# A third buffer for weight loads: taken over later, and its first load pinned in the queue

## The chip, the cores and the metric

The kernel runs on one core of a Trainium2 chip. The metric is the device time of one execution in microseconds. It is given as the median of several runs. One further execution was taken with the hardware profiler, and every row shown here comes from it.

## What is computed

One step of a hybrid encoder layer for 1024 prompt tokens and 32 sample tokens that share all weights, with model width 1024. Cut to the main lines, the reference is

```python
h = rms_norm(x, g_mix)
q, k, v, ch, cb, cc, ga, gb = split(h @ w_in)
a = window_attention(q, k, v) @ w_attn_out
bo = (cb * causal_conv3(cc * ch)) @ w_conv_out
x = x + (sigmoid(ga) * a + sigmoid(gb) * bo) @ w_mix_out
x = x + cross_attention(rms_norm(x, g_cross) @ w_cq, mem_k, mem_v) @ w_co
x = x + square(relu(rms_norm(x, g_mlp) @ w_up)) @ w_down
y = rms_norm(x, g_final)
```

with outputs for the new keys, values, convolution states and memory keys and values beside `y`.

## The kernel before

**Layout.** Activations lie transposed: 128 features on the partitions, tokens along the free axis. The 1056 tokens are three chunks of 384, 384 and 288. A weight is used in blocks of 128 x 1024 floats (512 KB). Every operand is split into a high and a low part, and a product is three matmuls (high x high, high x low, low x high), so a block of 1024 x 128 weights against one chunk of 384 columns is 24 matmuls.

**How a weight comes in.** `fetch_w` (line 145) takes a raw tile and issues the load on SyncE (line 155); `issue_w` (line 158) has ScalarE cast it into `wh` (line 129 in the profile, the line of a helper's `act.copy`) and VectorE subtract to get `wl` (line 130). `wh` and `wl` have three tiles each, the raw tile `wr` has two. `next_w` keeps three weights ready when an item of the plan asks for one, so a weight is cast at most when the third weight before it has been used up. `worder` is the order of all weights, written down while the plan is made. Odd-numbered weights of conv_out, mix, cq and co have their low part stored to DRAM (line 172, `wl_d`) the first time and loaded again (line 166) for the later chunks, where only the cast (line 167) is done anew.

**The third raw tile.** While the dictionary `third` is filled, each third fetch goes into a tile `ws` of another pool instead of `wr`. In the gate stage (`gate_pair`, line 908) that pool is `Y["top"]`. After the gates it is `W["pool"]`, whose only tile is also one of the two buffers of the weight sums:

```python
if third:
    third["n"] += 1
if third and third["n"] % 3 == 0:
    raw = third["pool"].tile([P, 4, 256], F32, tag="ws", name=nm("wr3"))...
```

**The weight sums.** `sum_step` (line 702) runs on GpSimd: a piece of weights is loaded into `ws` or `xacc` by turns (line 712 or 714), four adds combine its quarters (line 719), and the sums are written to DRAM (`gsum_d`, `usum_d`, `wsum_d`; lines 723 to 725). The last pieces are parts of `w_up`, written to `usum_d`. All these steps come before `after_gates` in the plan.

**Stages around the change.** First come seven gate pairs, f from 1 to 7, each with the weights w_in 34+f, two g_sum blocks and w_in 42+f. Then `after_gates` (line 1018) fills `third` anew with the count 0. Then comes the list `trunks[0]`: conv_out 0 to 7 of chunk 0, conv_out 0 of chunk 1, and mix 0 to 7 of chunk 0. `beside` (line 1630) puts these items into the plan one by one, with extra calls after chosen items. Then follow the rest of chunk 1 beside the cross-attention of chunk 0, and so on. `do_conv_out` (line 1042) loads a part `m1_d` (line 1046), adds on GpSimd (line 1051) and splits the result for mix. `do_mix` (line 1057) loads x (line 1061) and adds it (line 1065). `mem_load` (line 1094) loads memory keys and values (lines 1076 and 1085). `open_late` empties `third` much later.

**What sets the order.** The order in which the engines get their instructions is not only the program's. A scheduler simulates the whole program while it is built and gives an engine the earliest instruction in the program whose data and tile it holds to be free at that moment; SyncE then issues its loads strictly in that order. `pin` marks an instruction: it may not be put ahead of the instruction that precedes it on its engine in the program.

Of the kernel before, what the change touches and what calls it, by code (L numbers as in the profile page):

```python
# [23 lines left out]
NF = 8  # L24
# [16 lines left out]
def hybrid_step(ctx: ExitStack, tc: tile.TileContext, io):  # L41
    nc = tc.nc
    act, dve, pool_e, pe, sp = nc.scalar, nc.vector, nc.gpsimd, nc.tensor, nc.sync
# [3 lines left out]
    def nm(s):  # L47
        uid[0] += 1
        return f"{s}_{uid[0]}"

    def opened(name, **kw):
        cm = tc.tile_pool(name=name, **kw)
        return cm, cm.__enter__()

    def closed(cm):
        cm.__exit__(None, None, None)
# [40 lines left out]
    def pin(ins):  # L97
        return tc.keep_in_program_order(ins)
# [6 lines left out]
    def tmp(n, dt=F32):  # L105
        return tp.tile([P, n], dt, tag="ct", bufs=NCT, name=nm("ct"))
# [11 lines left out]
    def item(fn, *keys):  # L118
        plan.append((fn, keys))
        worder.extend(keys)  # L120
# [11 lines left out]
    def weight(key):  # L132
        name, *at = key
        if name in ("w_down", "w_sum"):
            q, j, t = at
            return (wsum_d if name == "w_sum" else io[name])[j, t, :, :, q].rearrange("i p c -> p i c")
        if name == "g_sum":
            return gsum_d[at[0]][:, at[1]].rearrange("p h c -> p (h c)")
        src = io[name]
        for j in at:  # L140
            src = src[j]
        return src

    fetched = []
    third = {}

    def fetch_w():
# [3 lines that stand above are left out]
            raw = third["pool"].tile([P, 4, 256], F32, tag="ws", name=nm("wr3")).rearrange("p q c -> p (q c)")  # L151
        else:
            raw = wp.tile([P, 1024], F32, tag="wr", bufs=2, name=nm("wr"))
        src = weight(worder[wpos[0] + len(fetched)])
        sp.dma_start(raw.rearrange("p (i c) -> p i c", i=4) if len(src.shape) == 3 else raw, src)
        fetched.append(raw)

    def issue_w():
        if not fetched:
            fetch_w()  # L160
        raw = fetched.pop(0)
        key = worder[wpos[0]]
        hi = wp.tile([P, 1024], F32R, tag="wh", name=nm("wh"))
        lo = wp.tile([P, 1024], F32R, tag="wl", name=nm("wl"))
        if kept.get(key) is not None:
            sp.dma_start(lo.bitcast(F32), kept[key])
            act.copy(hi, raw)
        else:
            split(hi, lo, raw)
            if key in kept:  # L170
                kept[key] = dram.tile([P, 1024], F32, name=nm("wl_d"))
                sp.dma_start(kept[key], lo.bitcast(F32))
        ready.append((worder[wpos[0]], (hi, lo)))
        wpos[0] += 1
# [39 lines left out]
    def xacc_tile():  # L214
        xacc[0] = tp.tile([P, 1056], F32, tag="xacc", name=nm("xacc"))
        return xacc[0]
# [59 lines left out]
    W = {}  # L276
# [11 lines left out]
    def norm_x():  # L288
# [7 lines left out]
        def load_x():  # L296
            for c, (o, n) in enumerate(CH):
                raw = raw_tile()[:, : NF * n].rearrange("p (f t) -> p f t", f=NF)
                for h in range(4):
                    sp.dma_start(raw[:, 2 * h : 2 * h + 2], io[f"x{c}"][:, 2 * h : 2 * h + 2])  # L300
                    if c == h == 0:
                        sp.dma_start(prm, io["params"])
                        fetch_w()
                if c == 0:
                    fetch_w()
                    fetch_w()
                raws.append(raw)
# [427 lines left out]
    for i, h in enumerate(hosts):  # L735
        kv, p = i // 8, i % 8
# [54 lines left out]
    def pump(n):  # L791
        for into, at, t, get in coming:
            hi, lo = into[at] = (get(), get())
            pin(act.copy(hi, t))
            pin(dve.tensor_sub(lo, t, hi.bitcast(F32)))
        coming.clear()
        for into, at, src, cols, get in wanted[:n]:
            t = cols() if callable(cols) else tmp(cols)
            sp.dma_start(t, src)
            coming.append((into, at, t, get))  # L800
        del wanted[:n]
# [216 lines left out]
    def after_gates():  # L1018
        nonlocal m_cm, mpool, cr_cm, cr
        assert not pieces and "new" not in W  # L1020
        closed(x_cm)
        xacc_tile()
        third.update(n=0, pool=W["pool"])
        m_cm, mpool = opened("mpool", bufs=18, reuse_waits="tile")
        cr_cm, cr = opened("cross", bufs=1, reuse_waits="tile", side="right")

    item(after_gates)


# [583 lines left out]
    def cross_steps(c):  # L1613

        steps = [("call", [mem_load if c == 0 else mem_load_s])]
        steps.append(("call", [lambda: chunk_stats(c)]))
        steps.append(("items", [(do_cq(c, j), ("w_cq", j)) for j in range(2)]))
        for i, step in enumerate(cross_units(c)):
            steps.append(step)
            if i < 4 - c:  # L1620
                steps.append(("call", []))
        if c:
            steps.append(("call", []))
        steps.append(("items", [(do_co(c, 0), ("w_co", 0))]))
        steps.append(("items", [(do_co(c, 1), ("w_co", 1))]))
        if c == 0:
            steps.append(("call", [lambda: chunk_stats(c)]))
        return steps

    def beside(steps, fillers, late=()):  # L1630
        for i, filler in enumerate(fillers):
            item(*filler)
            for x in [x for at, x in late if at == i]:
                item(lambda x=x: x())
            if steps:
                kind, what = steps.pop(0)
                for x in what:
                    if kind == "items":
                        item(*x)
                    else:  # L1640
                        item(lambda x=x: x())
        return steps

    def trunk(c):
        return [(do_conv_out(c, f), ("w_conv_out", f)) for f in range(NF)] + [
            (do_mix(c, f), ("w_mix", f)) for f in range(NF)
        ]
# [3 lines left out]

    trunks = [trunk(c) for c in range(3)]
    trunks[0].insert(NF, trunks[1].pop(0))
    left = beside([], trunks[0], [(i, lambda: pump(2)) for i in range(NF)])
    item(lambda: pump(0))
    left = beside(cross_steps(0), trunks[1])

# [327 lines left out]
```

## Time and profile before

| | |
|---|---|
| median of 3 runs | 1779.99 us (1779.09 to 1783.26) |
| the profiled execution | 1778.09 us, its span 1776.3 us |
| TensorE busy | 1734.2 us, 98% |
| VectorE, ScalarE, GpSimd busy | 1184.4, 852.8 and 576.8 us |
| DMA | 349.75 MB, 197 GB/s in the mean |

Times of rows are counted from the start of the span. In a timeline row stand start, duration, engine and line, operation, tiles, and in brackets the idle time of the engine before it and what ended it. `SPq` is the SyncE queue. A row of busy times by stretch gives the stretch, its length, the busy time of PE, PEld (weight load into TensorE), DVE (VectorE), ACT (ScalarE) and POOL (GpSimd) with the number of instructions, then the granted TensorE clock, the busy share of the DMA engines and GB/s. A row of waits gives the waiting engine and line, what it waited for, and the total, count and longest in us.

### The profile page before, as it was taken

The numbers are of one execution on the slowest core, as the hardware profiler recorded it, in microseconds if no ns is written. First come the engines' busy times: TensorE is split into PE (matmuls) and PEld (weight loads), VectorE is DVE, ScalarE is ACT, GpSimd is POOL, SyncE is SP. The second block draws the span as 40 slices with busy tenths as digits, with TensorE's granted clock in tenths as the row PEclk, the third lists the DMA queues.
The fourth block names the chain that finished last, engine by engine and source line by source line (L and its number), as shares of the span: only waits on it lengthen the run. The fifth ranks groups of instructions, "written<-read, shape, count | busy, mean of one in ns | idle before, by whom it ended". The sixth has DMA issues, their size and how long they took to land.

```text
span 1776.3 us, 32569 instructions
## 1 busy us (share of the span) xinstructions
PE 1734.2 (98%) x12250; PEld 1716.3 (97%) x12250; DVE 1184.4 (67%) x2270; ACT 852.8 (48%) x1660; POOL 576.8 (32%) x651
## 2 busy tenths in 40 slices
PE   8999999999999999979999999999999999999998
PEld 8999999999999999979999989999999999999998
DVE  7776867868666647536667677786666686556575
ACT  8643534435335324324556665774444463333443
POOL 0025366543453444531225130004555510000121
PEclk9999999999999999989999998999999999999999
DMA  5333334333446888747765667575666686554554
GB/s 183 109 117 128 111 128 155 120 139 136 148 155 223 298 274 288 264 166 272 261 213 196 236 224 233 183 257 196 223 221 224 213 310 212 186 184 167 193 173 157
DMA packets 182221, 349.75 MB, mean 197 GB/s; under 512 B 19744, under 2 KB 102976, under 8 KB 181936
## 3 DMA queue, kind: packets, MB, share of 16 engines
q1 hardware_dynamic: 167008, 295.07, 49.1%
q0 software_dynamic: 15056, 52.60, 8.4%
q8 instruction: 96, 1.57, 0.4%
q14 instruction: 61, 0.50, 0.1%
HBM read 252.82 MB, written 94.19 MB: 195 GB/s over the span
## 4 chain that ended last, share of the span: by engine, by line
PE 77%; DMA 11%; POOL 6%; DVE 2%; issue 2%; ACT 2%; SPq 0%; DVEq 0%; POOLq 0%; ACTq 0%
PE acc L193 10%; PE acc L195 10%; PE acc L194 10%; PE acc L1772 6%; PE acc L1770 6%; PE acc L1771 6%; PE acc L864 5%; PE acc L866 5%; PE acc L865 5%; DMA wsum_d<-ws 3%; DMA wsum_d<-xacc 3%; POOL ws L719 2%; POOL xacc L719 2%; PE pc L864 2%; PE pc L865 2%
## 5 line engine op out<-in xcount | busy, mean ns | idle before, releaser
L129 ACT CAST wh<-wr 128x1024 fp32r<-128x1024 f32 x226 | 237.2, 1050 | 424.5 <-PE acc L1771 126.2
L130 DVE TENSOR_TENSOR wl<-wr,wh 128x1024 fp32r<-128x1024 f32 x226 | 292.5, 1294 | 140.6 <-ACT wh L129 138.6
L193 PE MATMUL acc<-X,wh 128*128 128x384 f32 (+1 forms) x864 | 281.8, 326 | 6.6 <-ACT wh L129 6.6
L194 PE MATMUL acc<-X,wh 128*128 128x384 f32 (+1 forms) x864 | 279.1, 323 | 0.0
L195 PE MATMUL acc<-X,wl 128*128 128x384 f32 (+1 forms) x864 | 278.5, 322 | 0.3 <-DVE wl L130 0.3
L269 POOL TENSOR_TENSOR xacc<-xacc,ct 128x384 f32<-128x384 f32 (+1 forms) x56 | 73.4, 1314 | 401.8 <-ACT ct L267 400.3
L193 PEld LDWEIGHTS acc<-X,wh 128*128 128x128 f32 x864 | 163.0, 189 | 7.2 <-ACT wh L129 6.6
L194 PEld LDWEIGHTS acc<-X,wh 128*128 128x128 f32 x864 | 163.1, 189 | 0.7
L195 PEld LDWEIGHTS acc<-X,wl 128*128 128x128 f32 x864 | 162.8, 188 | 0.9 <-DVE wl L130 0.8
L195 PE MATMUL acc<-Y,wl 128*128 128x384 f32 (+1 forms) x432 | 139.1, 323 | 1.8 <-DMA wl<-wl_d 1.8
L193 PE MATMUL acc<-Y,wh 128*128 128x384 f32 (+1 forms) x432 | 138.8, 323 | 0.4 <-ACT Y L774 0.4
L194 PE MATMUL acc<-Y,wh 128*128 128x384 f32 (+1 forms) x432 | 139.1, 322 | 0.0
L1770 PE MATMUL acc<-n,wh 128*128 128x264 f32 x352 | 100.2, 285 | 0.0
L1771 PE MATMUL acc<-n,wh 128*128 128x264 f32 x352 | 100.1, 284 | 0.0
L1772 PE MATMUL acc<-n,wl 128*128 128x264 f32 x352 | 100.0, 285 | 0.1
L129 ACT CAST PTh<-pt 128x512 fp32r<-128x512 f32 (+3 forms) x94 | 46.0, 516 | 111.6 <-PE pt L582 110.8
L719 POOL TENSOR_TENSOR ws<-ws 128x256 f32<-128x256 f32 x100 | 91.9, 919 | 5.6
L719 POOL TENSOR_TENSOR xacc<-xacc 128x256 f32<-128x256 f32 x100 | 87.9, 879 | 5.5 <-DMA xacc<-in_w_in 0.2
L195 PEld LDWEIGHTS acc<-Y,wl 128*128 128x128 f32 x432 | 81.1, 188 | 2.1 <-DMA wl<-wl_d 2.1
L193 PEld LDWEIGHTS acc<-Y,wh 128*128 128x128 f32 x432 | 80.9, 188 | 0.7 <-ACT Y L774 0.7
L194 PEld LDWEIGHTS acc<-Y,wh 128*128 128x128 f32 x432 | 81.1, 188 | 0.0
L864 PE MATMUL acc<-n,wh 128*128 128x264 f32 x256 | 72.9, 285 | 0.8 <-DVE Z L1502 0.8
(422 smaller groups left out, 5511.5 us busy)
## 6 DMA issues: line engine op xcount, KB each, us to landing
wr<-in_w_in SPq DMA_DIRECT2D x53, 512.0 KB, 3.7
wr<-in_w_up SPq DMA_DIRECT2D x53, 512.0 KB, 4.5
wr<-wsum_d SPq DMA_DIRECT2D x40, 512.0 KB, 3.4
wr<-in_w_conv_out SPq DMA_DIRECT2D x24, 512.0 KB, 4.3
wr<-in_w_mix SPq DMA_DIRECT2D x24, 512.0 KB, 4.8
wr<-in_w_down SPq DMA_DIRECT2D x24, 512.0 KB, 3.4
wl<-wl_d SPq DMA_DIRECT2D x18, 512.0 KB, 4.6
n_d<-Z SPq DMA_DIRECT2D x32, 264.0 KB, 4.3
```

The costliest lines, as they stand in the source:

```text
L129: act.copy(hi, src)
L130: dve.tensor_sub(lo, src, hi.bitcast(F32))
L193: pe.matmul(out, wh[:, a], hi, start=(k == 0), stop=False)
L194: pe.matmul(out, wh[:, a], lo, start=False, stop=False)
L195: pe.matmul(out, wl[:, a], hi, start=False, stop=(k == len(acts) - 1))
L719: pin(pool_e.tensor_tensor(t[:, to], t[:, x], t[:, y], op=ALU.add))
L864: pe.matmul(acc, wh[:, a], hi, start=(start and k == 0), stop=False, skip_group_check=True)
L865: pe.matmul(acc, wh[:, a], lo, start=False, stop=False, skip_group_check=True)
L866: pe.matmul(acc, wl[:, a], hi, start=False, stop=(k == 3), skip_group_check=True)
L1770: pe.matmul(a, wh[:, s], hi, start=(t == 0 and k == 0), stop=False, skip_group_check=True)
L1771: pe.matmul(a, wh[:, s], lo, start=False, stop=False, skip_group_check=True)
L1772: pe.matmul(a, wl[:, s], hi, start=False, stop=(t == 1 and k == 7), skip_group_check=True)
```

## The change

`after_gates` no longer fills `third`. It is filled, with the count 0, by an extra call behind the item of index 12 in `trunks[0]`, which is mix 3 of chunk 0. The first load into the third tile of that pool, fetch number 3 of the new count, is pinned. Up to mix 3 all fetches use the two `wr` tiles.

```diff
@@ fetch_w
-        sp.dma_start(raw.rearrange("p (i c) -> p i c", i=4) if len(src.shape) == 3 else raw, src)
+        load = sp.dma_start(raw.rearrange("p (i c) -> p i c", i=4) if len(src.shape) == 3 else raw, src)
+        if third and third["n"] == 3 and third["pool"] is W["pool"]:
+            pin(load)
         fetched.append(raw)
@@ after_gates
         xacc_tile()
-        third.update(n=0, pool=W["pool"])
         m_cm, mpool = opened("mpool", bufs=18, reuse_waits="tile")
@@ the plan
     trunks[0].insert(NF, trunks[1].pop(0))
-    left = beside([], trunks[0], [(i, lambda: pump(2)) for i in range(NF)])
+    left = beside(
+        [], trunks[0], [(i, lambda: pump(2)) for i in range(NF)] + [(12, lambda: third.update(n=0, pool=W["pool"]))]
+    )
```

## The prediction

> **What bounds the kernel now.** I read the page first (engine shares), then the busy times by stretch to find where TensorE is not full, then the timelines of PE, ACT, SyncE and VectorE there, the waits of the SyncE queue, and the chain that ended last.
>
> ```profile
> PE 1734.2 (98%) x12250; PEld 1716.3 (97%) x12250; DVE 1184.4 (67%) x2270; ACT 852.8 (48%) x1660; POOL 576.8 (32%) x651
> 740.00:750.00 10.00, 10.00 (x63) 10.00 (x62) 3.79 (x5) 1.77 (x3) 5.82 (x7) 1.00 0.68 223
> 776.33:785.70 9.37, 0.00 (x0) 0.00 (x0) 0.02 (x1) 1.09 (x2) 0.16 (x1) 0.60 0.77 253
> 785.70:791.97 6.27, 6.27 (x21) 6.15 (x22) 5.24 (x7) 4.33 (x7) 0.00 (x0) 0.50 1.01 339
> 785.70 0.69 PE L864 MATMUL acc<-X,wh 128*128 128x384 f32 x1 [9.38 <-ACT wh L129]
> 784.61 1.05 ACT wh L129
> ```
>
> TensorE is the bound (98%), so only its gaps and its slow stretches can be won. The largest gap is 9.4 us, at 776.3 to 785.7, and it ends when ScalarE has cast a weight. In the rows by stretch, the number behind the engines is the granted clock: it is 0.50 for the 6.27 us after the gap. Why was that weight late?
>
> ```profile
> 752.34 0.33 SPq L155 DMA_DIRECT2D wr<-in_w_in  x1
> 778.99 0.33 SPq L155 DMA_DIRECT2D wr<-in_w_conv_out  x1
> 779.42 0.38 SPq L155 DMA_DIRECT2D wr<-in_w_in  x1
> 780.37 0.38 SPq L155 DMA_DIRECT2D wr<-gsum_d  x1
> 781.75 0.46 SPq L155 DMA_DIRECT2D wr<-gsum_d  x1
> ...
> SPq L155 <- DMA ws<-in_w_up: 16.3, 2, 15.4
> SPq L155 <- DMA usum_d<-ws: 9.8, 1, 9.8
> ...
> 775.77 3.10 DMA usum_d<-ws
> ...
> 753.56 1.73 DVE L130 TENSOR_TENSOR wl<-wr,wh 128x1024 fp32r<-128x1024 f32 x1
> ```
>
> SyncE issues nothing from 752.7 to 778.99. What it then issues is a conv_out weight, ahead of the w_in and g_sum weights that the last gate pair needs sooner. That load waited (15.4 + 9.8 us in the waits of the queue) for the weight-sum buffer `ws`: first the fetch of the last up piece into it, then the write of its sums, which lands at 778.87. So it is the first third-buffer load. Counting the fetches after the gates (conv_out 3, 4, 5 of chunk 0 are numbers 1, 2, 3), it carries conv_out 5, due some 50 us later on TensorE. The scheduler put it on the in-order queue before the gate loads; behind it stood the weights of gate pair 7 and the a_d/m1_d transfers. The w_in weight itself had a buffer long before: by the gate pairs' own count of three it goes into the gate stage's third tile, whose last reader is the 753.56 row, so it could have left at 755.3 and landed some 16 us before the gap.
>
> **The change part by part.** *Third buffer off until after mix 3.* Fetches of conv_out 3 to mix 5 all use the two `wr` tiles. A `wr` load can't be issued before the split of two weights earlier has read the tile, so conv_out 5 can't stand ahead of the gate weights, and nothing else on SyncE in this stretch waits for the sums. Removed: the gap, 9.4 us, and the slow clock behind it. 21 matmuls took 6.27 us there; at the rate of the row 740 to 750 (63 in 10 us) they take 3.33, so 2.9 us more. Together 12.3 us. What would be late next in the gates? The two g_sum weights go into `wr` tiles, the later of which is free at 765.0 (row below), w_in 49 follows them, and GpSimd's sums end at 778.9 whatever TensorE does; its first following add is at 814.87 (row below), 802.6 when shifted. I see nothing up to the end of the gates.
>
> The Trainium skill (TensorE: Matmul & The Clock Gate, Part 1) says that about 3.4 us of sustained work brings the full clock back. The trace shows 6.27 us at half rate, so it disagrees here. By the page the slow stretch would be worth 1.7 us, and the gain some 1.2 us smaller; the trace decides.
>
> ```profile
> 763.79 1.23 DVE L130 TENSOR_TENSOR wl<-wr,wh 128x1024 fp32r<-128x1024 f32 x1 [2.75 <-ACT wh L129]
> ```
>
> *Two buffers instead of three for ten weights* (conv_out 5 to 7, the first of chunk 1, mix 0 to 5). I place each load on the time axis of before.
>
> ```profile
> 809.77 0.34 PE L193 MATMUL acc<-Y,wh 128*128 128x384 f32 x1
> 813.97 0.34 PE L193 MATMUL acc<-Y,wh 128*128 128x384 f32 x1
> DMA to landing us min/median/max: 3.8/4.8/6.1
> 816.87 1.23 DVE L130 TENSOR_TENSOR wl<-wr,wh 128x1024 fp32r<-128x1024 f32 x1 [2.14 <-ACT wh L129]
> 823.59 1.05 ACT L129 CAST wh<-wr 128x1024 fp32r<-128x1024 f32 x1
> 858.65 1.05 ACT L129 CAST wh<-wr 128x1024 fp32r<-128x1024 f32 x1
> 859.74 1.23 DVE L130 TENSOR_TENSOR wl<-wr,wh 128x1024 fp32r<-128x1024 f32 x1 [0.53 <-ACT wh L129]
> 861.37 0.42 SPq L155 DMA_DIRECT2D wr<-in_w_mix  x1
> 862.71 1.04 ACT L129 CAST wh<-wr 128x1024 fp32r<-128x1024 f32 x1
> 874.92 1.04 ACT L129 CAST wh<-wr 128x1024 fp32r<-128x1024 f32 x1
> 861.02 0.44 PE L195 MATMUL acc<-M,wl 128*128 128x384 f32 x1 [0.52 <-DVE wl L130]
> 878.49 0.44 PE L195 MATMUL acc<-M,wl 128*128 128x384 f32 x1 [0.45 <-DVE wl L130]
> 884.69 0.45 PE L195 MATMUL acc<-Y,wl 128*128 128x384 f32 x1 [1.77 <-DMA wl<-wl_d]
> ```
>
> TensorE takes a weight in 4.2 us (809.77 to 813.97). A tile's round is the landing (median 4.8 us), the cast 1.05 and the split 1.23: 7.1 us, under the 8.4 that two tiles allow. Conv_out 5 takes conv_out 3's tile, free at 818.1: issued then, landed 822.9, cast at 823.59 as before. Its followers chain in the same way: the first of chunk 1 and mix 0 are cast 1 to 1.5 us later than before and still some 5 us ahead of need. The tight one is mix 5. ScalarE casts mix 3 only at 858.65 (it stands behind copies of the memory values), the tile is free at 860.97, the load leaves at 861.37 (the place that mix 6 had), lands 866.2, is split by 868.5, against 862.71 for its cast before. TensorE reaches it at 809.77 + 14 x 4.21 + 0.5 = 869.2. It is 0.7 us early by the median landing and 0.6 late by the longest, 6.1. Mix 7 then takes mix 5's tile, lands 873.7, ahead of its cast at 874.92, which already cost 0.45. I charge 0.6 us. Lower end 0; upper end: one landing too many exposed at mix 5, 4.8 us.
>
> *The pinned load* is fetch 3 of the new count, conv_out 1 of chunk 1, the same weight that has a third tile now. It is held behind mix 5's x load, the sixth of that line.
>
> ```profile
> 866.32 0.43 SPq L155 DMA_DIRECT2D wr<-in_w_conv_out  x1
> 875.72 0.59 SPq L1061 DMA_DIRECT2D ct<-in_x  x1
> 814.87 1.00 POOL L1051 TENSOR_TENSOR ct<-ct,ct 128x384 f32<-128x384 f32 x1 [38.38 <-DMA mkr<-mk_d]
> 1000.00:1225.00 225.00, 211.78 (x1574) 205.52 (x1573) 169.76 (x341) 140.50 (x310) 33.52 (x31) 0.96 0.65 219
> ```
>
> It moves from 866.32 to about 876.3 and lands at 881.1, cast by 882.2. TensorE comes to it at 882.3 and then waits anyway until 884.69 for the kept low half, which is loaded from DRAM into `wl`. Cost 0, cover 2.4 us; if the cover goes, up to 4.2 (one weight's time). Its buffer was free some 85 us before (778.9 against 876.3, shifted by the 12.3), so the wait on the sums is gone; queued behind it on SyncE are mix 6's and 7's x loads and the kept low half, for which VectorE's adds and TensorE wait.
>
> *Everything after* is the same program, but the order on each engine is made anew by the scheduler. The stretch 1000 to 1225 has 13.2 us of idle TensorE (225 less 211.78), which hang on such order. I take a quarter of it, 3 us, to either side and 0 as the value, as nothing in the change speaks for a sign.
>
> Sum: -12.3 + 0.6 = -11.7 us. The profiled execution took 1778.09 us (span 1776.3), so 1766.4. The median of the runs shown is 1.9 above that execution, so I forecast 1768.3.
>
> **The rivals.** *Partly eaten (no change that can be measured).* Two pieces of the chain that ended last:
>
> ```profile
> 834.91 0.19 PE acc L195
> 884.69 0.45 PE acc L195
> ```
>
> The chain that ended last leaves TensorE at 834.9 and comes back only at 884.69, over SyncE loads of m1_d, memory values and x. If this SyncE order, and not TensorE, sets the mix stage, two buffers make SyncE wait oftener and the chain longer. With mix 5 (4.8) and the pinned load (4.2) both exposed, less the 0.6 counted, the sum is -3.3: 1776.7. For it: the three small waits there (0.52, 0.45 and 1.77 us) show no slack. Against: conv_out and the early mixes have some 5 us.
>
> *Slower: two buffers starve TensorE.* If a round takes over 8.4 us, each weight from conv_out 5 to mix 7 (12) costs half the excess, after the 5 us lead is used up. Break-even is 12 x (r/2 - 4.2) = 12.3 + 5, a round of 11.3 us. At 13 us it is 27.6 - 5 = 22.6, net +10.3: 1790.3. For it: a cast held as long as at 858.65 (its `wh` tile was free when TensorE ended mix 0, at 851.9, so 6.7 us earlier) makes a round near 14, and DMA is 0.89 busy from 815 to 840:
>
> ```profile
> 815.00:840.00 25.00, 25.00 (x146) 25.00 (x145) 19.14 (x29) 14.24 (x25) 6.26 (x5) 1.00 0.89 306
> ```
>
> Against: that hold occurs once, and 6.1 is the longest landing of 15. The Trainium skill (Perfetto Trace Analysis, Optimization Strategy) speaks for this rival: gaps that repeat can mean too few buffers for the next tile. The trace of before has no repeating gap in this stretch, only the three waits.
>
> *It does nothing.* Another load could be put ahead of the gate weights and block at the same place: 1780. I see no other SyncE instruction that waits for the sums' buffers.
>
> **How the numbers follow.** Forecast 0.70, partly eaten 0.13, slower 0.14, nothing 0.03. The likeliest alone spans -12.3 - 3 = 1764.7 to 0.6 + 4.2 + 3 above 1768.3, some 1774. A measurement here can tell about 0.3%, 5.3 us: faster is below 1774.7, slower above 1785.3. A few of the partly eaten cases end below 1774.7, so faster 0.72, same 0.14, slower 0.14. The range takes in the partly eaten and the null case: 1763.5 to 1783, with most of the slower rival left out.
>
> **What would show it.** Right: no SyncE silence near 752 to 779; TensorE full and the clock at 1.00 from 755 to the end of the gates; conv_out 0 starting near 797.5 instead of 809.77; no conv_out 5 load before gate pair 7's weights; mix 5 within 1 us of its weight; the pinned load not waiting for GpSimd. Wrong: waits of TensorE on `wh` or `wl` at several weights in a row between conv_out 5 and mix 7 (the slower rival), a new long silence on SyncE, or a gap of over 4 us at conv_out 1 of chunk 1 behind the pinned load.

## The result, and the profile after

The changed kernel takes 1767.36 us (median of 4, 1765.48 to 1769.03) against 1780.03 us before (the median of four runs, the three of above and one more): the ratio is 0.9925, with a 95% interval of 0.9908 to 0.9943. A second comparison, beside the last experiment, gave 0.9949 (0.9931 to 0.9967). The forecast was 1768.3 us, a ratio of 0.993. The profiled execution took 1767.1 us, with a span of 1765.3 us against 1776.3, so 11.0 us less.

The weight loads on the SyncE queue of the changed kernel, in order of time, over the stretch in which the queue of the kernel before was silent (the transfers of other lines between them are left out):

```profile
754.62 3.19 SPq L155 DMA_DIRECT2D wr<-in_w_in  x2
760.17 0.33 SPq L155 DMA_DIRECT2D wr<-gsum_d  x1
767.33 0.32 SPq L155 DMA_DIRECT2D wr<-gsum_d  x1
775.93 0.33 SPq L155 DMA_DIRECT2D wr<-in_w_in  x1
778.44 0.33 SPq L155 DMA_DIRECT2D wr<-in_w_conv_out  x1
```

The busy times of the changed kernel in two windows (the window, its length, the busy time and count of PE, PEld, DVE, ACT and POOL, and then the granted clock, the DMA share and GB/s):

```profile
750.00:800.00 50.00, 50.00 (x313) 50.00 (x312) 25.47 (x35) 17.82 (x27) 19.82 (x22) 1.00 0.60 204
776.33:785.70 9.37, 9.37 (x62) 9.37 (x61) 4.98 (x7) 3.22 (x6) 3.98 (x5) 1.00 0.63 212
```

And GpSimd in order of time, its last write of the sums and its next work that waits for something:

```profile
779.42 1.45 POOL L725 DMA_DIRECT2D usum_d<-ws  x2 [0.41 <-POOL ws L721]
804.63 1.00 POOL L1052 TENSOR_TENSOR ct<-ct,ct 128x384 f32<-128x384 f32 x1 [23.76 <-DMA mkr<-mk_d]
```

The gate weights now leave one after another as their tiles come free, and no conv_out load stands between them. TensorE is full from 750 to 800 at a clock of 1.00; the 9.37 us that held nothing before hold 62 matmuls. The sums still end about where they did (their last write is issued at 779.42), but nobody waits for them.

Four instructions that both kernels have cut the span into stages: the first transpose of the window attention, the first conv_out matmul, the first score matmul of the cross-attention, and the first matmul of the down projection that reads a tile `n`. Three of them are read from the first start of a group, which is the number before "to"; the numbers ahead of it are the shortest, median and longest duration in ns. The groups of before:

```profile
L582 PE MATMUL pt<-ident,S x248: 270/272/329, 99.7 to 542.8; 128*128 128x128 f32 x124
L1140 PE MATMUL sc<-mkh,Y x36: 274/280/387, 910.5 to 1136.7; 128*128 128x256 f32 x36
L1770 PE MATMUL acc<-n,wh x352: 279/284/367, 1436.1 to 1763.1; 128*128 128x264 f32 x176
```

The same groups of after, and its first conv_out matmul from the timeline (799.53; it is 809.77 before):

```profile
L584 PE MATMUL pt<-ident,S x248: 270/272/330, 101.7 to 544.7; 128*128 128x128 f32 x124
799.53 0.34 PE L195 MATMUL acc<-Y,wh 128*128 128x384 f32 x1
L1141 PE MATMUL sc<-mkh,Y x36: 274/280/387, 901.7 to 1126.9; 128*128 128x256 f32 x36
L1773 PE MATMUL acc<-n,wh x352: 279/284/367, 1425.5 to 1752.2; 128*128 128x264 f32 x176
```

| stage, us | before | after | difference |
|---|---|---|---|
| start to the first transpose | 99.7 | 101.7 | +2.0 |
| to conv_out 0 | 710.1 | 697.8 | -12.2 |
| to the first cross-attention score | 100.7 | 102.2 | +1.4 |
| to the first matmul of down on `n` | 525.6 | 523.8 | -1.8 |
| to the end of the span | 340.2 | 339.8 | -0.4 |
| span | 1776.3 | 1765.3 | -11.0 |

The whole gain arises ahead of conv_out 0. The start is the same program in both; its 2.0 us are a difference between two executions.

### The profile page after: what moved, and what is told of

Same layout as the page of the kernel before. It is cut to its first block, busy times and chain, and to the rows that moved or that the text cites. A ratio compares the mean times of both kernels' runs of the same rounds, so it can differ in the third digit from the quotient of the medians.

```text
span 1765.3 us, 32571 instructions
## 1 busy us (share of the span) xinstructions
PE 1730.6 (98%) x12250; PEld 1713.2 (97%) x12250; DVE 1186.7 (67%) x2270; ACT 853.7 (48%) x1660; POOL 575.6 (33%) x651
## 4 chain that ended last, share of the span: by engine, by line
PE 50%; DMA 5%; DVE 3%; ACT 2%; issue 1%; POOL 0%; SPq 0%; DVEq 0%; POOLq 0%; ACTq 0%
PE acc L1773 6%; PE acc L1775 6%; PE acc L1774 6%; PE acc L866 6%; PE acc L868 6%; PE acc L867 6%; PE pc L866 2%; PE pc L867 2%; PE pc L868 2%; PE acc L197 2%; PE acc L195 2%; PE acc L196 2%; DMA ct<-m_d 1%; DVE wl L130 1%; DMA wr<-in_w_conv_out 1%
## 5 line engine op out<-in xcount | busy, mean ns | idle before, releaser
L130 DVE TENSOR_TENSOR wl<-wr,wh 128x1024 fp32r<-128x1024 f32 x226 | 296.1, 1310 | 133.4 <-ACT wh L129 131.5
```

The source lines that it names most:

```text
L130: dve.tensor_sub(lo, src, hi.bitcast(F32))
```

## The experiments

Ratios are to the kernel before, run on the same chip.

**The pin alone.** The takeover stays where it was, in `after_gates`. From the kernel before, its main lines:

```diff
+        load = sp.dma_start(...)
+        if third and third["n"] == 3 and third["pool"] is W["pool"]:
+            pin(load)
```

> The third tile is taken over at the old place, right after the gates; only the pin on its first load (conv_out 5 of chunk 0) is added. Queue theory: what costs is the place of that one load ahead of the last gate pair's weights on SyncE; the pin alone removes the silence of SyncE, the 9.4 us gap and the half clock, and no weight loses its third tile. 1765 to 1768 us, as the changed kernel or up to 1 us better. Rival (taking the tile over too early is what costs, wherever the load stands): still about 1780.

1767.8 us, ratio 0.9935 (0.9911 to 0.9959): not to be told from the changed kernel. The pin alone gives the gain. The pinned load itself came late. The SyncE row and TensorE's wait in this kernel:

```profile
815.50 0.33 SPq L155 DMA_DIRECT2D wr<-in_w_conv_out  x1
822.48 0.45 PE L195 MATMUL acc<-Y,wh 128*128 128x384 f32 x1 [2.37 <-ACT wh L129]
```

Conv_out 5 was loaded behind conv_out 6 and 7, and TensorE waited 2.4 us for it.

**The move alone.** The takeover behind mix 3, without the pin. From the changed kernel:

```diff
-        if third and third["n"] == 3 and third["pool"] is W["pool"]:
-            pin(load)
```

> The takeover moved behind mix 3, without the pin. Queue theory: the first load into the tile, now conv_out 1 of chunk 1, is free to go ahead as soon as the scheduler's simulation holds the tile free, so it stands at the same place ahead of gate pair 7's weights as the load of conv_out 5 did, and waits for the same sums: SyncE silent to about 779, the gap of 9 us and the half clock are back, 1778 to 1782 us. Rival (the move is what helps, the pin is a detail): 1766 to 1769.

1779.72 us, ratio 1.0003 (0.9989 to 1.0018): the move alone gives nothing. The queue and TensorE:

```profile
754.09 0.33 SPq L155 DMA_DIRECT2D wr<-in_w_in  x1
780.54 0.33 SPq L155 DMA_DIRECT2D wr<-in_w_conv_out  x1
780.98 0.38 SPq L155 DMA_DIRECT2D wr<-in_w_in  x1
787.21 0.69 PE L864 MATMUL acc<-X,wh 128*128 128x384 f32 x1 [9.14 <-ACT wh L129]
```

The silence, the gap and the half clock behind it are all back. The load in the bad place is now conv_out 1 of chunk 1, which TensorE needs 100 us later: the order in which the scheduler gives out loads looks at the free tile, not at the need.

**One more piece of sums, in the kernel before.** The last up piece is loaded, summed and written a second time. From the kernel before:

```diff
+    pieces += [("u", 1, 1)]
...
     item(close_gates)
     item(sum_step)
+    item(sum_step)
```

> The kernel before with one more piece of weight sums at the end: the last up piece is loaded, summed and written a second time with the same values. Queue theory: the sums end one step, about 10 us, later, SyncE comes free near 789 instead of 779, the gap grows from 9.4 to about 19 us, 1788 to 1792 us. Rival (the gain of the change came from a changed order in general, or from DMA traffic, not from this wait): within 2 us of 1780.

1784.78 us, ratio 1.0033 (1.0021 to 1.0044). It is slower, as the theory says and the rival does not, but by 5.3 us instead of 10. The trace shows why:

```profile
760.35 0.33 SPq L155 DMA_DIRECT2D wr<-gsum_d  x1
791.22 0.33 SPq L155 DMA_DIRECT2D wr<-in_w_conv_out  x1
791.66 0.36 SPq L155 DMA_DIRECT2D wr<-gsum_d  x1
798.90 0.69 PE L865 MATMUL acc<-X,wh 128*128 128x384 f32 x1 [14.36 <-ACT s L943]
```

SyncE comes free 12 us later, but the scheduler had also moved the load back by two weights (the w_in block and one g_sum block of gate pair 7 now stand ahead of it), so TensorE had more to do before it starved. The gap is 14.4 us instead of 9.4, so 5.0 more. Against that, the stretch at half clock behind it is 2.7 us shorter (3.61 against 6.27, rows in the last section), which is worth about half of that, 1.3 us. In the profiled executions the stage up to conv_out 0 is 4.0 us longer (714.1 against 710.1) and the span 3.8; the medians differ by 5.3.

**The same piece in the changed kernel.**

> The changed kernel with the same additional piece of sums. Queue theory: nothing waits for the sums any more before GpSimd's first add of conv_out 0 near 804, the sums end near 791, so 1767 to 1768.5 us, as without the piece. Rival (the end of the sums still sets the pace at the end of the gates): 1775 or more.

1769.56 us, ratio 0.9943 (0.9922 to 0.9964). That is 1.1 us more than I had expected at most, but the interval overlaps that of the changed kernel (0.9908 to 0.9943), and the rival's 1775 is far off. The sums end later and cost nothing, since GpSimd is next asked for at 803:

```profile
789.29 1.45 POOL L726 DMA_DIRECT2D usum_d<-ws  x2 [0.41 <-POOL ws L722]
803.36 1.00 POOL L1054 TENSOR_TENSOR ct<-ct,ct 128x384 f32<-128x384 f32 x1 [12.62 <-DMA wr<-in_w_conv_out]
```

**No third tile after the gates.** From the kernel before:

```diff
-        third.update(n=0, pool=W["pool"])
```

> No third tile at all after the gates: two raw tiles from conv_out 3 of chunk 0 to the end of the first weight stages. No load stands ahead of the gate weights, so the gap at 776 is gone. Own working (a tile's round of 7.1 us fits into the 8.4 us that two tiles allow): waits of one or two us at single weights in the later chunks, 1766 to 1774 us. Rival of the prediction (two buffers starve TensorE): waits at many weights in a row, 1785 us or more.

1775.81 us, ratio 0.9981 (0.9969 to 0.9993). The gap at 776 is gone, but about two thirds of the gain is gone too; the range of my working was missed by 2 us. The starving rival did not come true either. Of TensorE's waits from 950 to 1250, with two tiles, the three longest and the longest on a weight:

```profile
PE acc L193 <- DVE Z L1296: 6.0, 1, 6.0
PE acc L864 <- ACT lt L1353: 2.6, 2, 2.1
PE acc L193 <- DVE Ga L1064: 2.4, 1, 2.4
PE acc L864 <- ACT wh L129: 1.2, 1, 1.2
```

and the two longest in the changed kernel:

```profile
PE acc L866 <- ACT lt L1325: 2.4, 1, 2.4
PE acc L195 <- DVE Ga L1066: 1.9, 1, 1.9
```

TensorE does not wait at many weights in a row: waits on weights come to 1.2 us and 0.2 us there. One new wait of 6.0 us near 1090 stands out. So the third tile is worth some 8 us (1775.81 against 1767.36), and since the changed kernel too has two tiles for the ten weights from conv_out 5 to mix 5, it is worth them later on. The rows of the stage from the first cross-attention score to the first matmul of down on `n`, first the changed kernel, then this one:

```profile
901.70:1425.50 523.80, 510.27 (x3875) 504.35 (x3874) 369.83 (x630) 294.10 (x549) 182.26 (x139) 0.99 0.66 220
906.60:1435.30 528.70, 509.45 (x3875) 503.83 (x3874) 375.12 (x630) 294.36 (x549) 183.04 (x139) 0.98 0.67 219
```

Here the stage is 4.9 us longer, and TensorE is idle for 19.3 us of it instead of 13.5. How two tiles lead to the one long wait was not traced.

**The takeover behind conv_out 2, pinned.** From the changed kernel, the part of the line that differs:

```diff
-[(12, lambda: third.update(n=0, pool=W["pool"]))]
+[(2, lambda: third.update(n=0, pool=W["pool"]))]
```

> The changed kernel with the takeover behind conv_out 2 instead of mix 3, first load (conv_out 7) still pinned: conv_out 7, mix 1 and mix 4 get the third tile. If two tiles cost the charged 0.6 us or up to 5 in this stretch, 1762 to 1767 us; if the stretch has slack, as the working says, no difference: 1766 to 1768.5. Rival (the late takeover itself is what helps): slower, 1772 or more.

1766.91 us, ratio 0.9934 (0.9913 to 0.9955), the same as the changed kernel. The pinned load is conv_out 7 here, and it is late by more than in the first experiment:

```profile
827.45 0.33 SPq L155 DMA_DIRECT2D wr<-in_w_conv_out  x1
833.22 0.69 PE L195 MATMUL acc<-Y,wh 128*128 128x384 f32 x1 [4.75 <-ACT wh L129]
```

The loads of conv_out 0 of chunk 1 and of mix 0, which come behind it in the program, went ahead of it. The stage from conv_out 0 to the first cross-attention score is 3.7 us longer than in the changed kernel (105.9 against 102.2), but the next is 3.5 shorter (520.3 against 523.8), and the span of this execution, 1764.8 us, is no longer: the 4.75 us are not seen at its end.

**Every third-tile load pinned.** From the changed kernel:

```diff
-        if third and third["n"] == 3 and third["pool"] is W["pool"]:
+        if third and third["n"] % 3 == 0 and third["pool"] is W["pool"]:
```

> The changed kernel with every third-tile load after the gates pinned, not only the first. Queue theory: only a load that waits for something late costs by its place; the later ones wait for a split that has long been done, so nothing to win, 1766 to 1769 us. Rival (loads placed ahead cost by their place alone, for instance by making the x and m1_d loads late): 1763 or less. Pinning can also make loads late behind x loads: up to 1775.

1787.21 us, ratio 1.0050 (1.0035 to 1.0066): some 20 us slower than the changed kernel, and outside all that I had expected. TensorE's four longest waits from 950 to 1250, and the row of the stage from the first cross-attention score to the first matmul of down on `n`:

```profile
PE acc L195 <- ACT wh L169: 3.9, 1, 3.9
PE sc L1141 <- ACT S L1146: 2.9, 2, 1.6
PE acc L195 <- ACT wh L129: 2.8, 1, 2.8
PE sc L1141 <- ACT mkh L129: 2.4, 1, 2.4
905.80:1446.40 540.60, 515.12 (x3874) 507.45 (x3873) 371.03 (x630) 294.29 (x549) 181.42 (x139) 0.98 0.65 214
```

Two of the longest are waits for weights (`wh`), which the changed kernel does not have there. The stage is 16.8 us longer than in the changed kernel (540.6 against 523.8), so most of the loss arises in it: TensorE is idle for 25.5 us of it instead of 13.5, and the granted clock is 0.98 in the mean instead of 0.99. So it helps that the later loads of this tile may go ahead, and holding back the first alone is enough. Which of the pinned loads cost how much was not traced.

**The load behind the gates, but not pinned among the conv_out weights.** From the kernel before, the main lines (`loads` keeps the load of each weight, and the bound lets this one go no earlier than behind that of conv_out 2):

```diff
-        sp.dma_start(...)
+        ...
+        if third and third["n"] == 3 and third["pool"] is W["pool"]:
+            with tc.issue_after(loads["w_conv_out", 2]):
+                load = sp.dma_start(into, src)
+        else:
+            load = sp.dma_start(into, src)
+        loads.setdefault(key, load.ins)
```

> The kernel before, takeover right after the gates; the first load into the tile (conv_out 5) may go ahead, but not ahead of the load of conv_out 2, the last weight asked for in the gates. It then stands near 797 us, 16 us behind the end of the sums and early for conv_out 5. Queue theory: the gap at 776 is gone, and so are the waits of 2 to 5 us that the pinned load made where it was pinned among conv_out weights; 1762 to 1767 us, level with or up to 5 us under the changed kernel. Rival (the stretch from conv_out to the cross-attention is set by other loads, its waits show up elsewhere): 1767 to 1770.

> The changed kernel once more on the same chip as the kernel with the load placed behind the gates, for the comparison: 1766 to 1769 us.

1770.45 us, ratio 0.9954 (0.9938 to 0.9971), beside 1770.13 us, ratio 0.9949 (0.9931 to 0.9967) for the changed kernel in the same rounds, itself 1.1 us above what I had expected: level. The up to 5 us that I had thought possible are not there, as the rival said. The load is issued early and without a wait:

```profile
797.27 0.33 SPq L159 DMA_DIRECT2D wr<-in_w_conv_out  x1
```

and TensorE has no wait of over 1.7 us between 740 and 960. That does not show at the end. No version found is faster than the changed kernel beyond the uncertainty.

## Why the prediction was right

*The load ahead of the gate weights.* Right, and shown from three sides: the pin alone removes the loss, the move alone keeps it, and lengthening the sums lengthens the gap in the kernel before and does nothing in the changed one.

*The term of 12.3 us.* Right in size: the stage up to conv_out 0 is 12.2 us shorter. That this is gap plus slow clock was read from the rows; 9.4 us of gap alone would leave 2.8 us without a cause. The extra piece of sums in the kernel before agrees with the sum: 5.0 us more gap less 1.3 us of slow clock is 3.7, and the stage grew by 4.0. The agreement to 0.1 us is luck, though: in seven other profiled executions without the gap the same stage took between 696.2 and 701.2 us.

*What removes it.* Here the prediction named the wrong half of the change. It said that the stall goes because conv_out 5 uses a `wr` tile. Conv_out 5 does, but in the kernel with the move alone the next user of the third tile took its place and the time stayed at 1779.72 us; the pin, which I booked as a cost with no benefit of its own, is what does it (1767.8 alone). "I see no other SyncE instruction that waits for the sums' buffers" held only because of the pin.

*Two tiles, 0.6 us.* Mix 5 came out nearly as worked. On the axis of after, 10.2 us earlier, its cast was due at 856.0 and TensorE at 859.0:

```profile
842.15 0.44 PE L195 MATMUL acc<-M,wh 128*128 128x384 f32 x1 [0.59 <-DVE ct L1051]
857.63 1.05 ACT L129 CAST wh<-wr 128x1024 fp32r<-128x1024 f32 x1 [4.24 <-DMA wr<-in_w_mix]
863.95 0.43 SPq L1062 DMA_DIRECT2D ct<-in_x  x1
864.70 0.33 SPq L155 DMA_DIRECT2D wr<-in_w_conv_out  x1
870.35 1.05 ACT L169 CAST wh<-wr 128x1024 fp32r<-128x1024 f32 x1 [2.89 <-DMA wr<-in_w_conv_out]
875.36 0.44 PE L197 MATMUL acc<-Y,wl 128*128 128x384 f32 x1 [2.59 <-DMA wl<-wl_d]
```

ScalarE waited 4.24 us for that weight and cast it at 857.63, 1.6 us later than worked, and TensorE did not wait for mix 5 at all. Its two longest waits in the stage are the 0.59 us at 842.15 and the 2.59 us at 875.36. The stage as a whole lost 1.4 us, of which 0.8 is a longer wait for the kept low half (2.59 against 1.77); the same kernel in its second comparison took 102.8 us for the stage, 0.6 more, so the 1.4 us are hardly clear of the difference between two executions.

*The pinned load at no cost.* Right: it leaves behind the sixth x load (863.95, then 864.70), is cast at 870.35, and TensorE would wait for the low half until 875.36 anyway. Where the pinned load is a conv_out weight of chunk 0 and has no such cover, TensorE waited for it: 2.4 and 4.75 us in two kernels above.

*The rivals.* Two tiles do not starve TensorE, neither here nor when they are kept for good, though that costs some 8 us (1775.81 against the 1790 of the rival). Partly eaten was right in kind only: the stage from conv_out to the cross-attention lost 1.4 us of the 12.2.

*The order made anew*, valued at 0 with 3 us to either side: the stage from the cross-attention to down gave 1.8 us.

*The number.* That the median lies 0.9 us from the forecast is in part luck. In the profiled executions the start, which the change does not touch, was 2.0 us longer, and the two stages behind the cross-attention 2.2 us shorter; and the same kernel gave a median of 1770.13 us in the second comparison. One bound in the working is 1.9 us too low: 0.6 + 4.2 + 3 above 1768.3 is 1776.1 and not 1774, which it is above the 1766.4 of the profiled execution. The range given does not hang on it.

## What to carry to other kernels

When a scheduler places loads by the moment at which it holds their tile to be free, a tile handed from one user to another is a risk: a load that is not needed for 50 us can stand at the head of an in-order queue and wait, with the urgent loads behind it. Look for a silent stretch of the queue and read which load ends it and what that load waited for; then hold back that one load, and leave the others free to run ahead. A bound that ties a load to the end of the wait is enough, and pinning more than that can cost more than the stall.

## What the runs showed that I had not expected

Gaps of TensorE of 2 to 5 us between conv_out and mix did not show at the end: a kernel with a 4.75 us gap there had a span of 1764.8 us, and kernels without it 1764.5 and 1765.3 us. The kernel with the 2.4 us gap had a span of 1769.5 us in its profiled execution, but that was the slowest of its four, and their median, 1767.8 us, is that of the changed kernel.

The stretch at half clock behind a gap has no fixed length. In the kernel before it lasted 6.27 us with TensorE busy all along. The Trainium skill (TensorE: Matmul & The Clock Gate, Part 1) gives about 3.4 us of sustained work, and the prediction took that for a disagreement. The same section of the Trainium skill says that the window in which activity is counted runs freely; if a whole busy window is needed, up to nearly two of them can pass (6.8 us, an estimate from that page of the Trainium skill), and 6.27 us fits. Two other kernels here have the gap end at another moment. The stretches behind it, first with the move alone, then with the extra piece in the kernel before:

```profile
787.21:792.31 5.10, 5.10 (x16) 4.98 (x17) 5.10 (x7) 4.08 (x7) 0.00 (x0) 0.50 0.97 351
798.90:802.51 3.61, 3.61 (x11) 3.61 (x12) 0.78 (x2) 0.00 (x0) 0.00 (x0) 0.50 0.75 288
```

At the end of each the granted clock is 1.00 again. So the same kind of gap was followed by 6.27, 5.10 and 3.61 us at half clock, all between one and two such windows. That agrees with the reading; three stretches do not prove it. The prediction's price of the slow clock, 2.9 us, holds for its own gap and not for every one.
